# The merge, the output projection and the top-64 of a transformer block: products moved from GpSimd to DVE, last chunks held back, three sorted lists merged

## Chip, cores and metric

The kernel runs on one core of a Trainium2 chip. The metric is the device time of one execution in microseconds (us), the median of several. The engines are named as the profile names them: PE multiplies matrices, DVE (VectorE) and ACT (ScalarE) work on tiles, POOL is GpSimd, SP issues most of the DMAs.

## What is computed

One layer of a diffusion backbone on 512 latent tokens of 1024 channels with 256 context tokens. Two attention branches are projected, gated, added and projected once more; then comes a layer norm, a router, and a mixture of 16 experts in which each expert takes its 64 best tokens.

```python
y = gates[..., :D_MODEL] * (o_mla @ w_o_mla) + gates[..., D_MODEL:] * (o_diff @ w_o_diff)
o_lat = y @ w_out
x = layer_norm(DEEPNORM_ALPHA * x + g1 * o_lat, ln1_g[l], ln1_b[l])
h = x * (1.0 + sc2) + sh2
aff = jax.nn.softmax((h @ w_router + b_router).astype(jnp.float32), axis=-1)
g, idx = lax.top_k(jnp.swapaxes(aff, 1, 2), cap)          # cap = 64 of 512 tokens, 16 experts
hid = silu(xe @ w1) * (xe @ w3);  ye = hid @ w2           # xe = h[idx], then ye * g is added back
x = layer_norm(DEEPNORM_ALPHA * x + g2 * moe, ln2_g[l], ln2_b[l])
```

## The kernel before

All products of the projections are made of three matmuls, since each operand is split into a high part and a rest (`mm3`, lines 80 to 84; `split`, lines 72 to 78: ACT writes the high part, DVE the rest). A scheduler puts the instructions of all engines in order, except PE's in the expert stage, where the order is the program's.

**The merge** (lines 897 to 912) walks over eight groups `j` of 128 channels. PE makes `om`, the MLA branch's projection, by 12 matmuls from `oM` and the split weights `ohi`, `olo`. DVE multiplies it with its gate into `gy` (L907). POOL adds the other branch, which lies gated in `th`, into `ys` (L909). ACT takes the high part `yh` (L910), DVE the rest `yl` (L911).

**The output projection** (lines 1001 to 1035) has two halves `hf` of 512 output channels, and in each four tiles `t` of 128 tokens. A tile is 24 matmuls into `po`: eight chunks `k` of the contraction, three matmuls each; chunk `k` needs `yh` and `yl` of group `k`. The weights come as `outraw`, and are split into `woh` and `wol` (`w_out_split`). In the first half DVE multiplies `po` with the modulation `g1b` into `r` (L1012) and adds the scaled residual into `xn` (L1013). In the second half POOL has multiplied the weights `outraw` with `g1b` before their split (L893), so DVE needs only L1013. `g1b` is spread over the partitions by two matmuls (L118) and two copies on ACT (L119). PE then transposes `xn` (L1016) and makes the router's logits `lgT` and `lg`; these stand in PE's order among the next tile's matmuls. In the second half each tile's chain goes on over DVE, POOL and ACT to its softmax `aff`.

**The top-64** (lines 985 to 1056): a tile's `aff` is transposed by PE to 16 rows, one for each expert (`columns`). `largest` takes eight rounds, each a MAX8 (the eight largest of a row, L989) and a MATCH_REPLACE8 that strikes them out (L991; the profile shows it with a MATCH_VALUE_LOAD ahead). Tiles 0 and 1 together make 256 columns, whose 64 largest are put ahead of the 256 columns of tiles 2 and 3; the second sort runs over these 320. The smallest of the 64 is the threshold; its broadcast `vb` (L1061) and two compares give the slots of the tokens, and the expert stage can begin.

**The expert stage** streams 201 MB of weights `moe_w` through a ring of pages in SBUF (`prefetch`, L941, issued by SP). A page is loaded again when PE has used it up. Some pages of the ring lie in memory that the merge and the projection use before.

Of the kernel before, what the change touches and what calls it, by code (L numbers as in the profile page):

```python
# [29 lines left out]
E_N = 16  # L30
# [8 lines left out]
MOD_AT = ((1, 4), (), (), (0, 1, 3), (0, 1, 3))  # L39
PARTS = (0, 384, 2), (384, 384, 2), (768, 256, 4)  # L40
BN_W = 128
T_SETS = ((0, 1), (2, 3))
D_PARTS, M_PARTS, D_TR, M_TR = 4, 4, 5, 1


# [7 lines left out]
def _layer(tc, A, out, opened):  # L53
# [835 lines left out]
        wraw[hf, kk] = raw  # L889

    def w_out_split(hf, kk):
        if hf:
            G.tensor_tensor(wraw[hf, kk], wraw[hf, kk], g1b[:, None, 512:].to_broadcast([128, 2, 512]), op=OP.mult)  # L893
        split(woh[hf][kk], wol[hf][kk], wraw.pop((hf, kk)))

    for c in range(2, 4):
# [3 lines left out]
    for c in range(4):  # L900
        hl = wos[c]
        for jj in range(2):
            j = 2 * c + jj
            ps = psc.tile([128, 512], F32, name="om", bufs=4)
            wo_mul(ps, hl, jj, oM)
            g = yt.tile([128, 512], F32, name="gy")
            V.scalar_tensor_tensor(g, th[j], 1.0, ps, op0=OP.add, op1=OP.mult)  # L907
            ys = yt.tile([128, 512], F32, name="ys")
            G.tensor_tensor(ys, g, th[KD + j], op=OP.add)  # L909
            S.activation(yh[:, j, :], ys, AF.Copy, scale=0.5)  # L910
            V.scalar_tensor_tensor(yl[:, j, :], ys, 0.5, f(yh[:, j, :]), op0=OP.mult, op1=OP.subtract)  # L911
        w_out_split(0, c)
# [53 lines left out]
    rM, _ = pool("rM", side="right")  # L966
    xn = [rM.tile([128, D], F32, name=f"xn{t}") for t in range(NT)]
    slt = rM.tile([128, NT, E_N], F32, name="slt")
    aff = rM.tile([128, NT, E_N], F32, name="aff")

    g1b = rM.tile([128, D], F32, name="g1b", tag="gb", bufs=1)
    for g in range(2):
        spread(g1b[:, g * 512:(g + 1) * 512], 0, 32 * g, psc.tile([128, 512], F32, name="om", bufs=4))
    mp, close_mp = pool("modp", side="left")
    for t in range(NT):
        dma(xn[t], xr[:, t, :])
# [3 lines left out]
    bst = [mp.tile([128, 2, 6], F32, name=f"bst{t}") for t in range(NT)]  # L980
    wrw = wrp.rearrange("p k e -> p (k e)")
    la0 = [mp.tile([128, E_N], F32, name=f"la{t}") for t in range(NT)]
    top = mp.tile([E_N, CAP], F32, name="top")

    def largest(src, w, dst, last=False):

# [6 lines left out]
    def columns(dst, c0, ts):

        ps = psc.tile([128, 512], F32, name="om", bufs=4)
        for i, t in enumerate(ts):
            T.transpose(ps[:E_N, i * 128:(i + 1) * 128], aff[:, t, :], ident)
            V.tensor_copy(dst[:, c0 + i * 128:c0 + (i + 1) * 128], ps[:E_N, i * 128:(i + 1) * 128])

    cand = [mp.tile([E_N, 128 * len(ts) + (CAP if i else 0)], F32, name=f"cand{i}") for i, ts in enumerate(T_SETS)]  # L1000
    for hf in range(2):
        hs = slice(hf * 512, (hf + 1) * 512)
        for t in range(NT):
            tsl = slice(t * 128, (t + 1) * 128)
            ps = psc.tile([128, 512], F32, name="po", bufs=2)
            for k in range(KD):
                mm3(ps, yh[:, k, tsl], yl[:, k, tsl],
                    woh[hf][k // 2][:, k % 2, :], wol[hf][k // 2][:, k % 2, :], k == 0, k == KD - 1)
            r = ps
            if hf == 0:  # L1010
                r = mp.tile([128, 512], F32, name="r", bufs=2)
                V.tensor_tensor(r, ps, g1b[:, hs], op=OP.mult)  # L1012
# [12 lines left out]
            lgs = mp.tile([128, 128], F32, name="lgs", bufs=1)
            S.activation(lgs, lgT[:, :128], AF.Copy)
# [12 lines left out]
            rsqrt(mv[:, 2:3], mv[:, 1:2], 1.0, 1)  # L1039
            V.scalar_tensor_tensor(la0[t], la0[t], mv[:, 2:3], brt, op0=OP.mult, op1=OP.add)  # L1040
            la = mp.tile([128, E_N], F32, name="la", bufs=2)
            V.scalar_tensor_tensor(la, lg[:, :E_N], mv[:, 2:3], la0[t], op0=OP.mult, op1=OP.add)
            sm_ = mp.tile([128, 4], F32, name="sm_", bufs=2)
            V.tensor_reduce(sm_[:, 0:1], la, axis=AX.X, op=OP.max, negate=True)
            S.activation(la, la, AF.Exp, bias=sm_[:, 0:1], accum_out=sm_[:, 1:2])
            V.reciprocal(sm_[:, 2:3], sm_[:, 1:2])
            V.tensor_scalar(aff[:, t, :], la, sm_[:, 2:3], None, op0=OP.mult)
            V.scalar_tensor_tensor(mv[:, 3:4], mv[:, 0:1], -1.0, mv[:, 2:3], op0=OP.mult, op1=OP.mult)
            G.tensor_scalar(xn[t], xn[t], mv[:, 2:3], mv[:, 3:4], op0=OP.mult, op1=OP.add)
            for i, ts in enumerate(T_SETS):  # L1050
# [6 lines left out]
    vb = psc.tile([128, 512], F32, name="om", bufs=4)  # L1060
# [293 lines left out]
```

## Time and profile before

| | us |
|---|---|
| median of 3 runs (1062.12 to 1064.32) | 1063.86 |
| the profiled execution's own time | 1062.01 |
| its span | 1060.2 |
| PE busy, DVE busy, ACT busy, POOL busy | 981.3, 451.9, 277.9, 201.5 |
| merge begins on PE, projection's last matmul begins, expert stage's first matmul begins | 465.37, 555.45, 572.15 |

Busy times are sums over the whole span; an engine can be busy and still wait at the place that counts. The times of single instructions are counted from the span's start. "[9.37 <-DVE xn L1013]" behind an instruction means that its engine was idle for 9.37 us before it and that the named instruction ended the wait.

### The profile page before, as it was taken

The numbers are of one execution on the slowest core, as the hardware profiler recorded it, in microseconds if no ns is written. First come the engines' busy times: TensorE is split into PE (matmuls) and PEld (weight loads), VectorE is DVE, ScalarE is ACT, GpSimd is POOL, SyncE is SP. The second block draws the span as 40 slices with busy tenths as digits, with TensorE's granted clock in tenths as the row PEclk, the third lists the DMA queues.
The fourth block names the chain that finished last, engine by engine and source line by source line (L and its number), as shares of the span: only waits on it lengthen the run. The fifth ranks groups of instructions, "written<-read, shape, count | busy, mean of one in ns | idle before, by whom it ended". The sixth has DMA issues, their size and how long they took to land.

```text
span 1060.2 us, 13786 instructions
## 1 busy us (share of the span) xinstructions
PE 981.3 (93%) x5267; PEld 617.0 (58%) x5267; DVE 451.9 (43%) x831; ACT 277.9 (26%) x555; POOL 201.5 (19%) x189
## 2 busy tenths in 40 slices
PE   6999998989989999998795999999999999999992
PEld 5888977768778777775563453535353534324331
DVE  2373366652678565547555413131313131111227
ACT  2222424224776555534110011010101001010010
POOL 2340020201667322226111500000000000000004
PEclk9999998999999999999896999999999999999996
DMA  9943346752112000047757979999999999999993
GB/s 296 310 145 117 91 142 238 239 185 61 29 32 65 31 20 2 20 138 273 272 203 306 337 302 409 409 409 409 409 409 409 409 409 409 409 409 408 409 373 119
DMA packets 101210, 266.97 MB, mean 252 GB/s; under 512 B 14021, under 2 KB 37529, under 8 KB 101145
## 3 DMA queue, kind: packets, MB, share of 16 engines
q1 hardware_dynamic: 100248, 264.52, 67.2%
q0 software_dynamic: 320, 1.05, 0.4%
q8 instruction: 41, 0.67, 0.3%
q10 hardware_dynamic: 576, 0.52, 0.1%
q14 instruction: 25, 0.20, 0.1%
HBM read 261.47 MB, written 2.10 MB: 249 GB/s over the span
## 4 chain that ended last, share of the span: by engine, by line
PE 66%; DMA 17%; DVE 8%; POOL 3%; issue 3%; ACT 2%; SPq 0%; POOLq 0%; DVEq 0%; ACTq 0%
PE h L1146 14%; DMA wr<-moe_w 12%; PE y L1162 9%; PE mx L1109 6%; PE acc L84 5%; PE acc L83 5%; PE acc L82 5%; PE sc L653 4%; DMA wa<-w_ada 4%; PE tpb L661 3%; PE av L841 2%; PE mx L1175 2%; PE tp L237 1%; PE av L777 1%; DVE wol L78 1%
## 5 line engine op out<-in xcount | busy, mean ns | idle before, releaser
L1146 PE MATMUL h<-wr,xe 128*64 128x512 f32 x1024 | 233.8, 598 | 8.8 <-DMA wr<-moe_w 7.1
L1146 PEld LDWEIGHTS h<-wr,xe 128*64 128x64 f32 x1024 | 68.2, 137 | 163.1 <-issue 106.5
L1162 PE MATMUL y<-wr,hidT 128*64 128x512 f32 x448 | 97.7, 594 | 0.0
L642 DVE TENSOR_REDUCE nm<-sc 128x1 f32<-128x768 f32 x64 | 61.0, 953 | 36.0 <-PE sc L653 35.5
L1121 POOL TENSOR_TENSOR oh<-oh,aff 128x512 f32<-128x512 f32 x8 | 8.4, 1047 | 353.2 <-PE mx L1109 353.2
L1149 DVE TENSOR_TENSOR hid<-hid,h 128x512 f32<-128x512 f32 x16 | 11.0, 687 | 145.6 <-PE h L1146 145.6
L1162 PEld LDWEIGHTS y<-wr,hidT 128*64 128x64 f32 x448 | 31.5, 137 | 61.8 <-issue 57.9
L643 ACT ACTIVATE P<-sc,nm 128x768 f32<-128x768 f32 x64 | 57.6, 900 | 31.9 <-DVE nm L642 22.9
L1109 PE MATMUL mx<-oh,xn 128*128 128x128 f32 x512 | 61.4, 283 | 1.4 <-DVE oh L1099 1.4
L1109 PEld LDWEIGHTS mx<-oh,xn 128*128 128x128 f32 x512 | 60.3, 199 | 2.5 <-issue 2.1
L75 ACT ACTIVATE whi<-wraw 128x1024 fp32r<-128x1024 f32 (+1 forms) x32 | 33.5, 1047 | 98.3 <-DMA wraw<-w_in 62.9
L78 DVE TENSOR_TENSOR wlo<-wraw,whi 128x1024 fp32r<-128x1024 f32 (+1 forms) x32 | 39.1, 1222 | 45.5 <-PE acc L83 30.0
L75 ACT ACTIVATE ye<-y 128x512 fp32r<-128x512 f32 (+2 forms) x17 | 9.7, 572 | 178.6 <-DVE y L1169 98.7
L82 PE MATMUL acc<-xlh,whi 128*128 128x512 f32 x128 | 50.9, 398 | 2.8 <-ACT whi L75 2.8
L1176 DVE TENSOR_TENSOR acc<-acc,mx 128x512 f32<-128x512 f32 x56 | 34.7, 680 | 41.4 <-PE mx L1175 41.4
L1148 ACT ACTIVATE hid<-h 128x512 f32<-128x512 f32 x16 | 9.6, 597 | 157.5 <-PE h L1146 157.5
L82 PE MATMUL acc<-whi,xlh 128*128 128x512 f32 (+1 forms) x128 | 49.6, 391 | 1.2 <-ACT whi L75 1.2
L83 PE MATMUL acc<-xll,whi 128*128 128x512 f32 x128 | 50.1, 391 | 0.0
L84 PE MATMUL acc<-xlh,wlo 128*128 128x512 f32 x128 | 49.5, 394 | 0.6 <-DVE wlo L78 0.5
L1169 DVE SCALAR_TENSOR_TENSOR y<-y,gate,g2b 128x512 f32<-128x512 f32 x14 | 9.9, 754 | 92.6 <-PE y L1162 92.6
L84 PE MATMUL acc<-whi,xll 128*128 128x512 f32 (+1 forms) x128 | 48.7, 381 | 0.5 <-POOL xll L78 0.5
L83 PE MATMUL acc<-wlo,xlh 128*128 128x512 f32 (+1 forms) x128 | 48.8, 381 | 0.1
(336 smaller groups left out, 1737.1 us busy)
## 6 DMA issues: line engine op xcount, KB each, us to landing
wr<-moe_w SPq DMA_DIRECT2D x372, 512.0 KB, 10.2
wa<-w_ada SPq DMA_DIRECT2D x32, 512.0 KB, 4.5
wraw<-w_in SPq DMA_DIRECT2D x28, 512.0 KB, 4.7
wa<-w_ada SPq DMA_DIRECT2D x8, 1024.0 KB, 9.2
wr<-moe_w SPq DMA_DIRECT2D x16, 384.0 KB, 8.5
outraw<-w_out SPq DMA_DIRECT2D x8, 512.0 KB, 10.2
xq<-x SPq DMA_DIRECT2D x4, 512.0 KB, 7.9
q<-q SPq DMA_DIRECT2D x16, 128.0 KB, 2.3
```

The costliest lines, as they stand in the source:

```text
L75: S.activation(hi, src, AF.Copy)
L78: (eng_lo or V).tensor_tensor(lo, src, f(hi), op=OP.subtract)
L82: T.matmul(ps, lh, rh, start=start, stop=False)
L83: T.matmul(ps, lh, rl, start=False, stop=False)
L84: T.matmul(ps, ll, rh, start=False, stop=stop)
L642: V.tensor_reduce(nm, ps[:, :768], axis=AX.X, op=OP.max, negate=True)
L643: S.activation(p, ps[:, :768], AF.Exp, bias=nm, accum_out=z)
L653: T.matmul(ps[:, a:b], l, r[:, a:b], start=i == 0, stop=i == len(passes) - 1)
L1109: T.matmul(pss[hf][:, kk * 128:(kk + 1) * 128], xn[t][:, k * 128:(k + 1) * 128], o[:, t].rearrange("p e s -> p (e s)"), start=t == 0, stop ...
L1146: T.matmul(ph[i][64 * hf:64 * hf + 64, :], xe[:, k, sl], w[:, hf * 512:(hf + 1) * 512], start=k == 0, stop=k == KD - 1)
L1162: T.matmul(py[hf][r0:r0 + 64, :], hT[:, e % 2, fc % 4, fc // 4, :], w[:, hf * 512:(hf + 1) * 512], start=fc == 0, stop=fc == KD - 1)
L1176: V.tensor_tensor(acc[t][:, hs], acc[t][:, hs], ps, op=OP.add)
```

## The change

POOL's two kinds of products go to DVE: `ys` (L909) becomes a DVE instruction, and the multiplication of the second half's weights by `g1b` (L893) is dropped, while all eight tiles now get the multiplication `r` when DVE takes them out of `po`. For the first two tiles PE multiplies chunks 0 to 6 of both, then spreads `g1b`, and only then does chunk 7 of each; `po` has three PSUM banks now and `om` three instead of four. The top-64 is made of three sorts instead of two: tiles 0 and 1 side by side (64 rows of 128 columns, two blocks of 32 rows, of which 16 are used), then tile 2 together with the 64 survivors of the first sort (192 columns), and tile 3 alone (128 columns). Two sorted lists of 64 are merged by the maximum of one list and the other read backwards: the 64 results are the 64 largest of both, in no order. The threshold is the smallest of the last merge (a TENSOR_REDUCE).

```diff
     def w_out_split(hf, kk):
-        if hf:
-            G.tensor_tensor(wraw[hf, kk], wraw[hf, kk], g1b[:, None, 512:].to_broadcast([128, 2, 512]), op=OP.mult)
         split(woh[hf][kk], wol[hf][kk], wraw.pop((hf, kk)))
...
-            G.tensor_tensor(ys, g, th[KD + j], op=OP.add)
+            V.tensor_tensor(ys, g, th[KD + j], op=OP.add)
...
-    aff = rM.tile([128, NT, E_N], F32, name="aff")
+    affp = rM.tile([128, NT, 32], F32, name="aff")
+    aff = affp[:, :, :E_N]
+    V.memset(affp[:, :, E_N:], 0.0)
...
-    for g in range(2):
-        spread(g1b[:, g * 512:(g + 1) * 512], 0, 32 * g, psc.tile([128, 512], F32, name="om", bufs=4))
...
+        if t == 1:
+            T.transpose(ps[:64, :128], affp[:, 0:2, :].rearrange("p t e -> p (t e)"), ident)
+            V.tensor_copy(cand01, ps[:64, :128])
+            largest(cand01, 128, l01)
+
+            S.activation(cand2[:, :CAP], l01[32:32 + E_N, ::-1], AF.Copy)
+            V.tensor_tensor(cand2[:, :CAP], cand2[:, :CAP], l01[:E_N], op=OP.max)
+            return
+        dst = cand2[:, CAP:] if t == 2 else cand3
+        T.transpose(ps[:E_N, :128], aff[:, t, :], ident)
+        V.tensor_copy(dst, ps[:E_N, :128])
+        if t == 2:
+            largest(cand2, CAP + 128, l2)
+        else:
+            largest(cand3, 128, l3, True)
...
+            if (hf, t) not in pos:
+                pos[hf, t] = psc.tile([128, 512], F32, name="po", bufs=3)
+                if (hf, t) == (0, 0):
+
+                    pos[0, 1] = psc.tile([128, 512], F32, name="po", bufs=3)
+                    for t_ in range(2):
+                        out_mul(pos[0, t_], 0, t_, range(KD - 1))
+                    for g in range(2):
+                        spread(g1b[:, g * 512:(g + 1) * 512], 0, 32 * g, psc.tile([128, 512], F32, name="om", bufs=3))
+                else:
+                    out_mul(pos[hf, t], hf, t, range(KD - 1))
+            ps = pos.pop((hf, t))
+            out_mul(ps, hf, t, range(KD - 1, KD))
+            r = mp.tile([128, 512], F32, name="r", bufs=2)
+            V.tensor_tensor(r, ps, g1b[:, hs], op=OP.mult)
             V.scalar_tensor_tensor(xn[t][:, hs], xn[t][:, hs], ALPHA, r, op0=OP.mult, op1=OP.add)
...
-    for i, ts in enumerate(T_SETS):
-        nxt_ = top if i + 1 == len(T_SETS) else cand[i + 1][:, 0:CAP]
-        largest(cand[i], 128 * len(ts) + (CAP if i else 0), nxt_, i + 1 == len(T_SETS))
+    V.tensor_tensor(l2, l2, l3[:, ::-1], op=OP.max)
+    top = mp.tile([E_N, 1], F32, name="top")
+    V.tensor_reduce(top, l2, axis=AX.X, op=OP.min)
```

The order that the scheduler makes of it moves at three places. First DVE from the end of the merge to the first tile taken out of `po` (numbers behind names tell buffers apart). Before:

```order
L907 SCALAR_TENSOR_TENSOR gy_4480<-th14_708,om_4467 128x512
L911 SCALAR_TENSOR_TENSOR yl_4296<-ys_4463,yh_4295 128x512
L911 SCALAR_TENSOR_TENSOR yl_4296<-ys_4482,yh_4295 128x512
L78 TENSOR_TENSOR wol_4520<-outraw_4517,woh_4519 128x1024
L78 TENSOR_TENSOR wol_4524<-outraw_4521,woh_4523 128x1024
L1012 TENSOR_TENSOR r_4617<-po_4592,g1b_4503 128x512
L78 TENSOR_TENSOR wol_4528<-outraw_4525,woh_4527 128x1024
L1013 SCALAR_TENSOR_TENSOR xn0_4497<-xn0_4497,r_4617 128x512
L78 TENSOR_TENSOR wol_4532<-outraw_4529,woh_4531 128x1024
```

And in the changed kernel:

```order
L904 SCALAR_TENSOR_TENSOR gy_4480<-th14_708,om_4467 128x512
L908 SCALAR_TENSOR_TENSOR yl_4296<-ys_4463,yh_4295 128x512
L906 TENSOR_TENSOR ys_4482<-gy_4480,th15_709 128x512
L908 SCALAR_TENSOR_TENSOR yl_4296<-ys_4482,yh_4295 128x512
L968 MEMSET aff_4502 128x4x16
L77 TENSOR_TENSOR wol_4515<-outraw_4512,woh_4514 128x1024
L77 TENSOR_TENSOR wol_4519<-outraw_4516,woh_4518 128x1024
L77 TENSOR_TENSOR wol_4523<-outraw_4520,woh_4522 128x1024
L77 TENSOR_TENSOR wol_4527<-outraw_4524,woh_4526 128x1024
L1042 TENSOR_TENSOR r_4641<-po_4588,g1b_4504 128x512
L1042 TENSOR_TENSOR r_4667<-po_4589,g1b_4504 128x512
L1043 SCALAR_TENSOR_TENSOR xn0_4497<-xn0_4497,r_4641 128x512
```

All four `wol` of the second half now stand ahead of the first `r`, and no product of POOL stands ahead of any of them. Second, PE around the transposes of the first tile of `xn`. Before they stand inside the second tile, behind 15 of its 24 matmuls:

```order
L82 MATMUL po_4641<-woh_4322,yh_4295 128x512
L83 MATMUL po_4641<-wol_4323,yh_4295 128x512
L84 MATMUL po_4641<-woh_4322,yl_4296 128x512
L1016 MATMUL om_4620<-ident_58,xn0_4497 128x128 x4
L82 MATMUL po_4641<-woh_4322,yh_4295 128x512
```

In the changed kernel they stand in the third tile (`po_4690`), behind 7 of its matmuls, and those of the second tile of `xn` follow at once:

```order
L83 MATMUL po_4589<-woh_4326,yl_4296 128x512
L81 MATMUL po_4690<-woh_4314,yh_4295 128x512
L82 MATMUL po_4690<-wol_4315,yh_4295 128x512
L83 MATMUL po_4690<-woh_4314,yl_4296 128x512
L81 MATMUL po_4690<-woh_4314,yh_4295 128x512
L82 MATMUL po_4690<-wol_4315,yh_4295 128x512
L83 MATMUL po_4690<-woh_4314,yl_4296 128x512
L81 MATMUL po_4690<-woh_4318,yh_4295 128x512
L1046 MATMUL om_4644<-ident_58,xn0_4497 128x128 x4
L1046 MATMUL om_4670<-ident_58,xn1_4498 128x128 x4
```

So PE has 16 matmuls more to do before it needs the first `xn`. Third, DVE at the end of the last tile, where the passes of the sorts stand between the chain's instructions. Before the last sort has DVE for itself:

```order
L1047 TENSOR_SCALAR aff_4502<-la_5034,sm__5036 128x16
L998 COPY cand1_4591<-om_5043 16x128
L989 MAX top_4589<-cand1_4591 16x8
L991 MATCH_REPLACE cand1_4591<-top_4589,cand1_4591 16x320
L989 MAX top_4589<-cand1_4591 16x8
```

In the changed kernel:

```order
L1077 TENSOR_SCALAR aff_4502<-la_5075,sm__5077 128x16
L985 MAX l01_4586<-cand2_4585 16x8
L1012 COPY cand01_4584<-om_5084 16x128
L987 MATCH_REPLACE cand2_4585<-l01_4586,cand2_4585 16x192
L985 MAX l3_4587<-cand01_4584 16x8
L985 MAX l01_4586<-cand2_4585 16x8
L987 MATCH_REPLACE cand01_4584<-l3_4587,cand01_4584 16x128
L987 MATCH_REPLACE cand2_4585<-l01_4586,cand2_4585 16x192
```

The second sort (`cand2`) is still under way when the last list (`cand01`, first 16 rows) arrives: its first five rounds and the sixth MAX stand between the instructions of the last tile's chain, the rest among the passes of the last list.

## Rows read from the trace of the kernel before

**Rows 1.** The chain of work that ended last (start us, us, what), expert stage.
```profile
855.05 4.21 PE h L1146 x19
859.26 10.18 DMA wr<-moe_w
```

**Rows 2.** Busy time by stretch: engines in us, granted clock of PE, DMA share, GB/s.
```profile
477.00:494.00 17.00, 16.77 (x72) 12.44 (x70) 13.79 (x16) 6.96 (x9) 9.17 (x6) 1.00 0.74 282
501.00:510.00 9.00, 1.08 (x5) 1.09 (x6) 8.96 (x7) 2.82 (x3) 6.18 (x2) 0.57 1.02 407
614.00:620.00 6.00, 6.00 (x57) 6.00 (x55) 1.52 (x5) 0.70 (x2) 0.11 (x1) 1.00 0.76 302
620.00:626.00 6.00, 6.00 (x27) 2.04 (x27) 1.21 (x4) 1.79 (x3) 0.94 (x1) 1.00 0.30 98
626.00:632.00 6.00, 6.00 (x32) 2.01 (x30) 0.00 (x0) 0.00 (x0) 0.00 (x0) 1.00 0.99 343
900.00:1033.00 133.00, 125.46 (x586) 46.55 (x582) 29.56 (x63) 11.68 (x23) 1.47 (x2) 1.00 1.03 402
```

**Rows 3.** Waits of PE, 463 to 640: us in total, times, longest.
```profile
PE om L1016 <- DVE xn L1013: 10.2, 2, 9.4
PE om L1061 <- DVE top L989: 8.5, 1, 8.5
...
PE po L84 <- DVE yl L911: 0.4, 1, 0.4
PE po L82 <- ACT yh L910: 0.2, 1, 0.2
```

**Rows 4.** Timeline of PE (start us, us), end of the merge and projection.
```profile
487.96 1.13 PE L118 MATMUL om<-rm,one 1*128 1x512 f32 x4
...
499.16 0.39 PE L84 MATMUL po<-woh,yl 128*128 128x512 f32 x1
508.92 1.11 PE L1016 MATMUL om<-ident,xn 128*128 128x128 f32 x4 [9.37 <-DVE xn L1013]
...
520.30 0.39 PE L83 MATMUL po<-wol,yh 128*128 128x512 f32 x1
520.52 0.39 PE L84 MATMUL po<-woh,yl 128*128 128x512 f32 x1
```

**Rows 5.** Groups by line, 463 to 580: xcount, busy us, mean ns, idle before.
```profile
L78 DVE TENSOR_TENSOR wol<-outraw,woh 128x1024 fp32r<-128x1024 f32 x8 | 16.4, 2067 | 3.9 <-ACT woh L75 3.9
...
L893 POOL TENSOR_TENSOR outraw<-outraw,g1b 128x1024 f32<-128x1024 f32 x4 | 11.3, 2856 | 1.7 <-ACT g1b L119 1.7
...
L989 DVE MAX8 top<-cand 16x8 f32<-16x320 f32 x8 | 3.9, 482 | 0.3
...
L989 DVE MAX8 cand<-cand 16x8 f32<-16x256 f32 x8 | 3.3, 413 | 0.1
...
L78 DVE TENSOR_TENSOR olo<-oraw,ohi 128x1024 fp32r<-128x1024 f32 x2 | 2.4, 1218 | 0.0
```

**Rows 6.** Timeline of DVE (start us, us), projection to the end of the sorts.
```profile
499.40 5.57 DVE L78 TENSOR_TENSOR wol<-outraw,woh 128x1024 fp32r<-128x1024 f32 x2 [3.85 <-ACT woh L75]
504.90 0.68 DVE L1012 TENSOR_TENSOR r<-po,g1b 128x512 f32<-128x512 f32 x1
...
514.04 0.69 DVE L1012 TENSOR_TENSOR r<-po,g1b 128x512 f32<-128x512 f32 x1 [0.62 <-PE po L84]
514.76 0.69 DVE L1013 SCALAR_TENSOR_TENSOR xn<-xn,r 128x512 f32<-128x512 f32 x1
...
520.95 0.69 DVE L1012 TENSOR_TENSOR r<-po,g1b 128x512 f32<-128x512 f32 x1 [2.44 <-PE po L84]
...
555.88 0.69 DVE L1013 SCALAR_TENSOR_TENSOR xn<-xn,po 128x512 f32<-128x512 f32 x1
...
561.41 0.48 DVE L989 MAX8 top<-cand 16x8 f32<-16x320 f32 x1
...
569.06 0.48 DVE L989 MAX8 top<-cand 16x8 f32<-16x320 f32 x1
```

More of the change, by code (lines that the diff above doesn't have):

```diff
@@ L41 @@
 BN_W = 128
-T_SETS = ((0, 1), (2, 3))
 D_PARTS, M_PARTS, D_TR, M_TR = 4, 4, 5, 1
@@ L903, in _layer @@
             j = 2 * c + jj
-            ps = psc.tile([128, 512], F32, name="om", bufs=4)
+            ps = psc.tile([128, 512], F32, name="om", bufs=3)
             wo_mul(ps, hl, jj, oM)
@@ L982, in _layer @@
     la0 = [mp.tile([128, E_N], F32, name=f"la{t}") for t in range(NT)]
-    top = mp.tile([E_N, CAP], F32, name="top")
     def largest(src, w, dst, last=False):
@@ L991, in largest, with columns, out_mul @@
                 V.match_replace(out=src[:, :w], in_to_replace=m8, in_values=src[:, :w], imm_value=-1.0)
[L993 to L1000, printed above, removed]
+    cand01 = mp.tile([64, 128], F32, name="cand01")
+    cand2 = mp.tile([E_N, CAP + 128], F32, name="cand2")
+    cand3 = cand01[:E_N]
+    l01 = mp.tile([64, CAP], F32, name="l01")
+    l2 = l01[:E_N]
+    l3 = mp.tile([E_N, CAP], F32, name="l3")
+    def columns(t):
+        if t == 0:
+            return
+        ps = psc.tile([128, 512], F32, name="om", bufs=3)
+        if t == 1:
[4 more added lines that the diff above has]
+            V.tensor_tensor(cand2[:, :CAP], cand2[:, :CAP], l01[:E_N], op=OP.max)
+            return
+        dst = cand2[:, CAP:] if t == 2 else cand3
[5 more added lines that the diff above has]
+            largest(cand3, 128, l3, True)
+    def out_mul(ps, hf, t, ks):
+        tsl = slice(t * 128, (t + 1) * 128)
+        for k in ks:
+            mm3(ps, yh[:, k, tsl], yl[:, k, tsl],
+                woh[hf][k // 2][:, k % 2, :], wol[hf][k // 2][:, k % 2, :], k == 0, k == KD - 1)
+    pos = {}
     for hf in range(2):
@@ L1003, in _layer @@
         for t in range(NT):
[L1004 to L1012, printed above, removed]
+            if (hf, t) not in pos:
[12 more added lines that the diff above has]
+            V.tensor_tensor(r, ps, g1b[:, hs], op=OP.mult)
             V.scalar_tensor_tensor(xn[t][:, hs], xn[t][:, hs], ALPHA, r, op0=OP.mult, op1=OP.add)
-            ps = psc.tile([128, 512], F32, name="om", bufs=4)
+            ps = psc.tile([128, 512], F32, name="om", bufs=3)
             for k in range(4):
@@ L1049, in _layer @@
             G.tensor_scalar(xn[t], xn[t], mv[:, 2:3], mv[:, 3:4], op0=OP.mult, op1=OP.add)
-            for i, ts in enumerate(T_SETS):
-                if ts[-1] == t:
-                    columns(cand[i], CAP if i else 0, ts)
-    for i, ts in enumerate(T_SETS):
-        nxt_ = top if i + 1 == len(T_SETS) else cand[i + 1][:, 0:CAP]
-        largest(cand[i], 128 * len(ts) + (CAP if i else 0), nxt_, i + 1 == len(T_SETS))
-    vb = psc.tile([128, 512], F32, name="om", bufs=4)
-    T.transpose(vb[:, :E_N], top[:, CAP - 1:CAP].to_broadcast([E_N, 128]), ident[:E_N, :E_N])
+            columns(t)
+    V.tensor_tensor(l2, l2, l3[:, ::-1], op=OP.max)
+    top = mp.tile([E_N, 1], F32, name="top")
+    V.tensor_reduce(top, l2, axis=AX.X, op=OP.min)
+    vb = psc.tile([128, 512], F32, name="om", bufs=3)
+    T.transpose(vb[:, :E_N], top.to_broadcast([E_N, 128]), ident[:E_N, :E_N])
     mk = mp.tile([128, NT, 2, E_N], BF16, name="mk")
@@ L1064, in _layer @@
         V.tensor_tensor(mk[:, :, i, :], aff, vb[:, None, :E_N].to_broadcast([128, NT, E_N]), op=op)
-    ps = psc.tile([128, 512], F32, name="om", bufs=4)
+    ps = psc.tile([128, 512], F32, name="om", bufs=3)
     pc = ps[:, :2 * NT * E_N].rearrange("p (t i e) -> p t i e", i=2, e=E_N)
```

## The prediction

> **What bounds the kernel now.** I read the chain of waits first. From 859 us on it goes over the loads of the expert weights [rows 1]: PE has caught up with the stream, and the kernel ends when the last page has landed and been used. The stream itself is read from the busy times by stretch: from 626 us to its end at 1033 us it is never idle, at a share of 0.99 and more and some 400 GB/s [rows 2]. Just ahead of that it has gaps: in 614 to 626 us its share is 0.76 and 0.30, so 1.4 + 4.2 = 5.6 us are idle, while PE is fully busy. There SP holds the next load until PE has used up a page. So the end hangs on the stream, the stream's last stop hangs on PE in the first expert pairs, and PE gets there by the path of this change: merge, projection, top-64. What this path gains, the releases of pages gain, and so the end, as long as the stream is not late already.
>
> Then the waits of PE on that path [rows 3]. Two are long: 9.4 us before the transposes of the first `xn`, and 8.5 us before the threshold's broadcast. The first is a wait behind others: PE has done 15 matmuls of the second tile at 499.5 us and then stands until 508.92 [rows 4], because the first `xn` on DVE stands behind `r`, and `r` behind two `wol` that take 5.57 us after a wait of 3.85 [rows 6] for ACT's `woh`, which in turn waits for POOL's products `outraw`. These take 2.86 us each, four in a row, and cannot begin before `g1b` is there; beside them a `wol` takes 2.07 us in the mean, where the same split `olo` takes 1.22 without POOL [rows 5].
>
> **The path's terms**, against the profiled execution's own 1062.0 us.
>
> *The wait of 9.4 us goes.* In the merge PE is not held up: 8 x 12 matmuls at 0.23 us (the spacing in [rows 4]) are 22.4 us from 465.4, so `om` ends at 488. Then come 42 matmuls (chunks 0 to 6 of two tiles, 9.8 us), the spread (1.1 us [rows 4], as before, only later) and 6 matmuls: the second tile is done near 500.4, and the 7 matmuls ahead of the first transposes last until 502.0. DVE needs, after its last `yl`, four `wol` of 1.22 us. I put the last `yl` at 493: `gy`, `ys`, ACT's `yh` and `yl` of the last group follow `om` by some 0.7 us each, and DVE has about 2 us of other splits still in hand. ACT's four `woh` run just ahead of the `wol`, so DVE is free at 498.5, and waits for PE. Then `r` and `xn` of tile 0 take 0.7 us each with the second `r` between them: 500.0 + 2.1 = 502.1, against PE's 502.0. Kept wait 0 to 1 us, I take 0.1. The cover is 1.5 us of DVE's idle time; what it costs if that is gone is rival A.
>
> *The slow clock behind it goes: -1.7.* In 501 to 510 us the granted clock is 0.57 [rows 2], which is 1.2 GHz for most of it, after PE had stood idle. From 508.92 to the next `r` at 514.04 are 9 matmuls and one tile's transposes and logits. At full clock a tile of 24 matmuls with them takes 520.95 - 514.04 = 6.91 [rows 6], so this piece would take 6.91 - 15 x 0.23 = 3.46 instead of 5.12.
>
> *The small waits go: -0.6.* PE waits 0.4 us for `yl` and 0.2 for `yh` [rows 3] at the last chunks of the first tile; now chunk 7 comes 11 us after `om`'s end.
>
> *Nothing for tiles 2 to 7.* DVE gets four more `r` (0.69 us each) in the second half, in tiles that take PE 6.9 us, and PE reaches a tile's transposes 7 matmuls into the next tile, 1.6 us after the tile's end; `r` and `xn` take 0.72 + 0.69 [rows 6]. That fits by 0.2 us; a pass of the sort between them eats it, at one tile.
>
> *The last tile: +0.7 and +1.0.* Behind the last matmul no cover is left. `r` ahead of `xn` costs its 0.72. The chain to the list's copy takes 561.41 - 555.88 = 5.5 us before. Now five rounds of the second sort stand in it. The bounds are 0 (they fill DVE's waits for PE, ACT and POOL) and their whole time. A round of 320 columns takes (569.06 - 561.41) / 7 = 1.09 us [rows 6]; MAX8 falls from 482 to 413 ns for 64 columns less [rows 5] and the strike-out alike, so a round of 192 is about 0.82 and one of 128 about 0.69, and five are 4.1 us at most. The chain's own waits are longer than that in sum, but a pass of 0.3 us begun just before a value arrives delays it. I take 1.0, nearer to 0.
>
> *The last sort: -0.5.* Before 8.1 us (561.41 to 569.54). Now 7 x 0.69 + 0.3 = 5.1, the leftover two and a half rounds of the second list 2.1, and the merge with the minimum 0.4: 7.6.
>
> The page "VectorE: DVE Perf Modes" of the Trainium skill (section on the TRN2 errata) says that a DVE instruction pays a fixed time whatever its length, and advises long ones. The rows have it: 482 against 413 ns leaves about 0.2 us when the columns are taken to nothing. If a short pass were no cheaper than one of 256 columns (0.96 a round by the same slope), the last term would be +1.8 instead of -0.5.
>
> Three sorts have 24 MAX8 where two had 16. The first, 8 x 0.69 = 5.5 us, runs between the chains of the seventh tile while PE multiplies on, 6.9 us to a tile, and costs nothing but the few tenths above; without that cover it would cost its 5.5.
>
> Sum: -9.4 + 0.1 - 1.7 - 0.6 + 0.7 + 1.0 - 0.5 = -10.4. The profiled execution would take 1051.6 us. The median shown is 1.9 above it, and the three runs spread over 2.2; I forecast **1052.5 us**, between 1051.6 and 1053.5. What a measurement of this kernel can tell from no change is about 0.2%, 2.1 us.
>
> **Rivals.**
>
> *A. DVE becomes the merge's bound (13 in 100).* In 477 to 494 us DVE is busy for 13.79 of 17 us [rows 2] and gets eight `ys` more. The Trainium skill ("Perfetto Trace Analysis", Optimizing Scalar/DVE Operations) says that work may be moved off a saturated DVE; this change moves it on. The rows have DVE at 0.81, near to that but not there. If DVE waits out each round trip to ACT (0.7 us, eight times), its 24 passes of 0.69, ten splits of 1.22 and these waits are 34.4 us from 468.5: `r` would begin at 503, `xn` come at 505, and PE wait 3 us and lose the clock for some 1.7: 1057. Against it: DVE's order has another group's pass to do during most of these trips, and POOL no longer stretches the splits.
>
> *B. The stream does not move in full (6 in 100).* If the earlier loads kept their times, only the 5.6 us of idle time before 626 us could be taken out: 1052.5 + 4.8 = 1057.3; if those gaps stayed too, 1062. Against it: the loads in them wait for PE, which is earlier.
>
> *C. The tail eats more (6 in 100).* All five rounds delay the last chain (+3.1) and short passes cost as long ones (+2.3): 1058.
>
> *D. Slower (3 in 100).* In the second half each `xn` comes late, PE stops in every tile, and the clock stays at 1.2 GHz, as it did after the stop at 499.5. With matmuls twice as long a tile would take 24 x 0.46 + 2 = 13 us, 6.1 more; two tiles eat the gain, six give 1052.5 + 37 = 1089. It decides by whether PE's wait in a tile grows from tenths to microseconds. Against it: from 510 us on PE runs without a stop with the same chain, less one pass.
>
> **Numbers.** The forecast has 72 in 100. A, B and C all end near 1057 and still faster; D and a stream that does not move at all (2 of B's 6) are not. The range has to hold the kept wait (0 to 1), the last tile's passes (0 to 4.1), the last sort (-0.5 to +1.8), the runs' spread of 2.2 and most of rival A: 1049.5 to 1057.5. Faster by more than 0.2% 0.95, within 0.2% 0.02, slower 0.03.
>
> **What would show it.** In the changed profile PE's wait for `xn` (9.4) is below 1 us and the clock near 500 us full; `wol` of the second half takes 1.2 us; `om` ends at 488 as before, the last projection matmul begins near 544 instead of 555.5, the broadcast near 559 instead of 569.6; the stream's last gap ends near 616 instead of 626, and the stream ends 10 us earlier. The forecast is wrong if PE still waits for more than 2 us before 510, if the broadcast follows the last matmul by more than 16 us (14.1 before), or if the stream's end moves by less than the broadcast.

## The result, and the profile after

The changed kernel takes **1049.65 us** (median of 4 runs, 1047.56 to 1050.75), the kernel before 1063.09 beside it (4 runs): a ratio of 0.9871, 95% interval 0.9851 to 0.989. By the ratio that is 13.7 us less. The forecast was 1052.5, between 1051.6 and 1053.5, in a range of 1049.5 to 1057.5. The gain came out some 2 to 3 us larger than forecast: the time lies below the narrower bounds and just inside the range. The two profiled executions (spans 1060.2 and 1045.8 us) differ by 14.4 us. Cut at the same places, in us, with a second profiled execution of the changed kernel (span 1046.4, from the experiments):

| stretch | before | forecast | after | after, 2nd |
|---|---|---|---|---|
| start to the merge's first matmul | 465.37 | 465.37 | 463.92 | 463.54 |
| to the projection's last matmul | 90.08 | 78.5 | 77.80 | 77.83 |
| to the copy of the last list | 5.65 | 7.35 | 7.73 | 7.39 |
| to the broadcast of the threshold | 8.50 | 8.0 | 6.89 | 6.90 |
| to the expert stage's first matmul | 2.55 | 2.55 | 2.58 | 2.59 |
| to its first product `h` | 6.87 | 6.87 | 5.76 | 6.67 |
| to the end | 481.18 | 481.18 | 481.12 | 481.48 |

The last row says that the whole gain of the path reaches the end. The waits of PE from 463 to 640 us, changed kernel (us in total, times, longest), beside [rows 3]:

```profile
PE om L1089 <- DVE top L1083: 6.9, 1, 6.9
PE om L1011 <- DVE aff L1077: 2.2, 1, 2.2
PE om L1046 <- DVE xn L1043: 1.6, 1, 1.6
```

The wait of 9.4 us before the first `xn` is gone, and so are those for `yl` and `yh`. What is left of the waits for `xn` (L1046) is the last tile's. The timeline of PE, changed kernel (start us, us):

```profile
463.92 0.50 PE L81 MATMUL om<-oM,ohi 128*128 128x512 f32 x1
...
486.42 0.39 PE L81 MATMUL po<-woh,yh 128*128 128x512 f32 x1
...
500.21 1.24 PE L1046 MATMUL om<-ident,xn 128*128 128x128 f32 x8
...
541.72 0.40 PE L83 MATMUL po<-woh,yl 128*128 128x512 f32 x1
543.75 0.66 PE L1046 MATMUL om<-ident,xn 128*128 128x128 f32 x4 [1.63 <-DVE xn L1043]
...
549.03 0.38 PE L1011 MATMUL om<-ident,aff 128*16 128x128 f32 x1 [2.21 <-DVE aff L1077]
556.34 0.28 PE L1089 MATMUL om<-ident,top 16*128 16x16 f32 x1 [6.93 <-DVE top L1083]
...
558.92 5.18 PE L1137 MATMUL mx<-oh,xn 128*128 128x128 f32 x32 [1.19 <-DVE oh L1127]
564.68 5.80 PE L1174 MATMUL h<-wr,xe 128*64 128x512 f32 x26 [0.57 <-DVE xe L1142]
```

PE stands nowhere between 463.92 and 541.72, the first transposes included. Behind the projection's last matmul its longest waits until the broadcast are those for `xn`, for `aff` and for the threshold `top`. The first 32 matmuls of the expert stage, `mx`, in the kernel before, from the stretch that the forecast left alone:

```profile
572.15 6.29 PE L1109 MATMUL mx<-oh,xn 128*128 128x128 f32 x32 [1.19 <-DVE oh L1099]
```

The same 32 matmuls took 6.29 us before and 5.18 after. DVE of the changed kernel, from the last `yl` to the threshold, beside [rows 6]:

```profile
490.73 0.69 DVE L908 SCALAR_TENSOR_TENSOR yl<-ys,yh 128x512 fp32r<-128x512 f32 x1 [0.70 <-ACT yh L907]
...
491.68 4.63 DVE L77 TENSOR_TENSOR wol<-outraw,woh 128x1024 fp32r<-128x1024 f32 x4 [0.19 <-ACT woh L74]
498.20 1.31 DVE L1042 TENSOR_TENSOR r<-po,g1b 128x512 f32<-128x512 f32 x2 [1.88 <-PE po L83]
...
549.45 0.28 DVE L1012 COPY cand<-om 16x128 f32<-16x128 f32 x1 [0.23 <-PE om L1011]
549.65 0.07 DVE L987 MATCH_VALUE_LOAD cand<-l,cand 16x8 f32 x1
549.72 0.33 DVE L987 MATCH_REPLACE8 cand<-l,cand 16x192 f32<-16x192 f32 x1
549.99 0.53 DVE L985 MAX8 l<-cand 16x8 f32<-16x128 f32 x2
...
552.07 0.27 DVE L985 MAX8 l<-cand 16x8 f32<-16x128 f32 x1
...
556.08 0.21 DVE L1083 TENSOR_REDUCE top<-l 16x1 f32<-16x64 f32 x1
```

Four `wol` now take 4.63 us together, where two took 5.57 [rows 6], and DVE has 1.88 us to spare before `r`. From 549.65 to 552.07 the rest of the second list's sort and two rounds of the last list alternate. Groups by line, 463 to 580 us, changed kernel (xcount, busy us, mean ns), beside [rows 5]:

```profile
L77 DVE TENSOR_TENSOR wol<-outraw,woh 128x1024 fp32r<-128x1024 f32 x8 | 9.4, 1219 | 0.2 <-ACT woh L74 0.2
L985 DVE MAX8 l<-cand 16x8 f32<-16x192 f32 x8 | 2.7, 338 | 0.0
L985 DVE MAX8 l<-cand 16x8 f32<-16x128 f32 x8 | 2.2, 278 | 0.2
```

The `wol` are back at the time of an undisturbed split, and MAX8 falls with the columns. Busy time by stretch, changed kernel (PE, PEld, DVE, ACT, POOL, PE's granted clock, DMA share, GB/s), beside [rows 2]:

```profile
477.00:494.00 17.00, 17.00 (x76) 13.80 (x75) 15.31 (x22) 10.49 (x13) 0.00 (x0) 1.00 0.75 270
501.00:510.00 9.00, 9.00 (x60) 6.45 (x62) 3.33 (x7) 2.17 (x5) 0.00 (x0) 1.00 1.03 410
557.00:561.00 4.00, 2.74 (x18) 2.61 (x19) 1.29 (x5) 0.00 (x0) 0.00 (x0) 0.50 1.03 410
561.00:565.00 4.00, 3.42 (x26) 3.11 (x27) 0.78 (x3) 1.28 (x1) 0.00 (x0) 0.90 0.70 279
...
602.00:606.00 4.00, 4.00 (x37) 3.83 (x36) 1.79 (x6) 0.06 (x1) 0.45 (x1) 1.00 0.51 205
606.00:610.00 4.00, 4.00 (x16) 1.32 (x18) 0.87 (x3) 1.73 (x3) 0.59 (x1) 1.00 0.10 15
610.00:614.00 4.00, 4.00 (x21) 1.29 (x18) 0.00 (x0) 0.00 (x0) 0.00 (x0) 1.00 0.92 320
```

The stream's last gap lies in 602 to 610 us, where before it lay in 614 to 626 [rows 2]: it moved with PE.

### The profile page after: what moved, and what is told of

Its sections match the earlier page's. It is cut to its first block, busy times and chain, and to the rows that moved or that the text cites. A ratio compares the mean times of both kernels' runs of the same rounds, so it can differ in the third digit from the quotient of the medians.

```text
span 1045.8 us, 13799 instructions
## 1 busy us (share of the span) xinstructions
PE 977.7 (93%) x5266; PEld 614.1 (59%) x5266; DVE 451.9 (43%) x870; ACT 278.2 (27%) x556; POOL 176.1 (17%) x177
## 3 DMA queue, kind: packets, MB, share of 16 engines
q0 software_dynamic: 320, 1.05, 0.4%
## 4 chain that ended last, share of the span: by engine, by line
PE 72%; DMA 16%; DVE 7%; ACT 2%; issue 2%; POOL 2%; SPq 0%; DVEq 0%; ACTq 0%; POOLq 0%
PE h L1174 16%; DMA wr<-moe_w 10%; PE y L1190 9%; PE mx L1137 6%; PE acc L83 5%; PE acc L82 5%; PE acc L81 5%; PE sc L652 4%; PE tpb L660 3%; DMA wa<-w_ada 3%; PE av L840 3%; PE mx L1203 2%; DMA wraw<-w_in 2%; PE tp L236 2%; PE po L83 1%
## 5 line engine op out<-in xcount | busy, mean ns | idle before, releaser
L74 ACT ACTIVATE whi<-wraw 128x1024 fp32r<-128x1024 f32 (+1 forms) x32 | 33.5, 1046 | 99.4 <-DMA wraw<-w_in 75.4
```

What stands on the lines that cost most here:

```text
L74: S.activation(hi, src, AF.Copy)
```

## The experiments

Times vary by 2 us and more from run to run, so each part is read from its stretch: *A* from the merge's first matmul to the projection's last (before 90.08, after 77.80 and 77.83 us), *B* from there to the broadcast (14.15; 14.62 and 14.29), *C* from the expert stage's first matmul to the first `h` (6.87; 5.76 and 6.67). Ratios are to the kernel before, with their 95% intervals.

### products_alone: the kernel before, with only the products moved

```diff
-        if hf:
-            G.tensor_tensor(wraw[hf, kk], wraw[hf, kk], g1b[:, None, 512:].to_broadcast([128, 2, 512]), op=OP.mult)
...
-            G.tensor_tensor(ys, g, th[KD + j], op=OP.add)
+            V.tensor_tensor(ys, g, th[KD + j], op=OP.add)
...
-            r = ps
-            if hf == 0:
-                r = mp.tile([128, 512], F32, name="r", bufs=2)
-                V.tensor_tensor(r, ps, g1b[:, hs], op=OP.mult)
+            r = mp.tile([128, 512], F32, name="r", bufs=2)
+            V.tensor_tensor(r, ps, g1b[:, hs], op=OP.mult)
```

> The kernel before with only the products moved: ys on DVE, no weights times g1b on POOL, r for all eight tiles; spread, tile order and both sorts as before. Theory (the products are the cause of the 9.4 us wait): the wait before the first xn shrinks to about 1 us, because three wol instead of four slow ones stand ahead of that xn; no slow clock near 500 us; from the last projection matmul to the broadcast 14.15 + 0.85 = 15.0 us, since r stands in the last tile's chain; the time is 1 to 2 us above the changed kernel, some 1051. Rival (holding back the last chunks is the cause): the wait stays at 4 us or more, the clock falls behind it, and the time is 1055 to 1058.

Measured: 1051.1 us, ratio 0.9901 (0.9876 to 0.9926); A 77.68, B 15.83. PE's timeline has no stop before the first `xn`, and its longest wait for `xn` is the last tile's:

```profile
499.33 0.66 PE L1012 MATMUL om<-ident,xn 128*128 128x128 f32 x4
...
546.32 0.66 PE L1012 MATMUL om<-ident,xn 128*128 128x128 f32 x4 [2.03 <-DVE xn L1009]
```

The products alone take away the whole of the long wait; the 1 us that I expected to be left is not there. B is 0.8 longer than expected, because passes of the 256-column sort stand in the last tile's chain: a MAX8 of 0.41 us ahead of `r`, a strike-out of 0.40 us with its load between `r` and `xn`.

### not_held: the changed kernel without the last chunks held back

```diff
+    for g in range(2):
+        spread(g1b[:, g * 512:(g + 1) * 512], 0, 32 * g, psc.tile([128, 512], F32, name="om", bufs=3))
...
-            if (hf, t) not in pos:
...
-            out_mul(ps, hf, t, range(KD - 1, KD))
+            ps = psc.tile([128, 512], F32, name="po", bufs=3)
+            out_mul(ps, hf, t, range(KD))
```

> The changed kernel without the last chunks held back: g1b is spread ahead of the projection, and the tiles of the first half are multiplied one after the other. Theory (with the products on DVE nothing is late any more, so holding back buys nothing): from the merge's first matmul to the last projection matmul 77.8 us, within 0.4 of the changed kernel; time within 1 us. Rival (it covers DVE's splits): PE waits 1 us or more for the first xn or for yl, 79 us or more.

Measured: 1048.38 us, ratio 0.9853 (0.9835 to 0.9872); A 78.02, B 14.61. Multiplying the last chunks behind is worth 0.2 us of A here, and nothing of the time. The rival falls.

### ys_on_pool and weights_on_pool: one product back on POOL

```diff
-            V.tensor_tensor(ys, g, th[KD + j], op=OP.add)
+            G.tensor_tensor(ys, g, th[KD + j], op=OP.add)
```

> The changed kernel with ys back on POOL. Theory (ys is no part of the gain): the last yl is 2 to 3 us later than in the changed kernel, four wol of 1.2 us follow, and PE waits 0.5 to 1.5 us for the first xn with the clock at its upper level; within 1.5 us of the changed kernel. Rival (ys on POOL stretches DVE's passes and is half of the gain): a wait of 3 us or more before the first xn, time 5 us above the changed kernel.

Measured: 1052.45 us, ratio 0.991 (0.9889 to 0.9932); A 80.31, B 15.05. A grew by 2.5 us, more than expected and at another place: PE stops not at the first `xn` but at the seventh chunk of the first tile (waits of PE):

```profile
PE po L81 <- ACT yh L907: 1.5, 1, 1.5
...
PE po L83 <- DVE yl L908: 0.4, 1, 0.4
```

From 488.71 us, the start of the matmul ahead of these two waits, to 492.06, that of the one behind them, are four steps: they take 3.35 us where four at 0.23 take 0.9, and these 2.4 us are nearly all of the 2.5. So the theory that `ys` is no part of the gain falls, and so does the rival's half of it.

```diff
+        if hf:
+            G.tensor_tensor(wraw[hf, kk], wraw[hf, kk], g1b[:, None, 512:].to_broadcast([128, 2, 512]), op=OP.mult)
...
-            r = mp.tile([128, 512], F32, name="r", bufs=2)
-            V.tensor_tensor(r, ps, g1b[:, hs], op=OP.mult)
+            r = ps
+            if hf == 0:
+                r = mp.tile([128, 512], F32, name="r", bufs=2)
+                V.tensor_tensor(r, ps, g1b[:, hs], op=OP.mult)
```

> The changed kernel, but POOL multiplies the second half's weights by g1b again, and r is made for the first half alone. Theory (the four products on POOL, which cannot begin before g1b, are the cause of the old wait, since wol and with them xn stand behind them on DVE): the first xn is on time, but a wol that waits for POOL stands ahead of the second xn; PE waits 2 to 4 us there, and the last tile is 0.85 us shorter without r; 1 to 4 us above the changed kernel. Rival (the last chunks held back are enough, since the second half's weights are due only at 525 us): no wait above 1 us, and the time is 1 us below the changed kernel's.

Measured: 1054.34 us, ratio 0.9929 (0.9906 to 0.9951); A 83.75, B 13.31. The timeline of POOL has the four products in one row:

```profile
498.26 11.27 POOL L892 TENSOR_TENSOR outraw<-outraw,g1b 128x1024 f32<-128x1024 f32 x4 [40.27 <-DMA xn<-x]
```

That of DVE shows what runs beside them:

```profile
499.29 1.92 DVE L1047 SCALAR_TENSOR_TENSOR xn<-xn,r 128x512 f32<-128x512 f32 x1
501.78 2.74 DVE L77 TENSOR_TENSOR wol<-outraw,woh 128x1024 fp32r<-128x1024 f32 x1 [0.57 <-ACT woh L74]
```

That of ACT shows `woh` waiting for POOL and `hT` behind it:

```profile
500.69 1.06 ACT L74 ACTIVATE woh<-outraw 128x1024 fp32r<-128x1024 f32 x1 [2.51 <-POOL outraw L892]
503.47 1.06 ACT L74 ACTIVATE woh<-outraw 128x1024 fp32r<-128x1024 f32 x1 [1.72 <-POOL outraw L892]
504.43 0.58 ACT L1052 ACTIVATE hT<-om 128x512 f32<-128x512 f32 x1
```

And that of PE two of the waits that follow, for `xn` and for `hT`:

```profile
501.26 0.66 PE L1050 MATMUL om<-ident,xn 128*128 128x128 f32 x4 [1.03 <-DVE xn L1047]
505.06 0.53 PE L1057 MATMUL lgT<-hT,wrg 128*32 128x128 f32 x8 [2.22 <-ACT hT L1052]
```

As expected the four products do the harm even with the chunks held back and the first `xn` on time, though by 6 us of A and not by 2 to 4, and in a way that I had not listed: ACT's `woh` waits for POOL, and `hT` stands behind it. A third wait for `xn`, of 0.80 us, comes at 515 us, and from 505 to 509 us the granted clock is 0.57. Beside POOL's product an `xn` of 0.69 us takes 1.92. The rows say how: this `xn` ends at 501.21 and the `wol` at 504.52, 0.52 and 1.05 us after the start of the `woh` that POOL's product released (500.69 and 503.47). The next `xn` and `wol` end 0.52 and 1.05 us after theirs as well. So these passes look held until POOL's product has ended, and not slowed in proportion; no run tests this by itself. B is 1.0 to 1.3 us shorter without the last tile's `r`, about the 0.85 expected.

With the chunks held back, taking `ys` back costs 2.5 us of A and taking the weights back 6.0, together 8.5 of the 12.3 us. How the rest divides between the two, and what holding the chunks back is worth while POOL still makes the products, no run shows.

### sorts_alone, two_sorts and one_after_another: the top-64

`sorts_alone` is the kernel before with the change's `columns` and merges; `two_sorts` is the changed kernel with the same piece taken back:

```diff
-    for i, ts in enumerate(T_SETS):
-        nxt_ = top if i + 1 == len(T_SETS) else cand[i + 1][:, 0:CAP]
-        largest(cand[i], 128 * len(ts) + (CAP if i else 0), nxt_, i + 1 == len(T_SETS))
+    V.tensor_tensor(l2, l2, l3[:, ::-1], op=OP.max)
+    top = mp.tile([E_N, 1], F32, name="top")
+    V.tensor_reduce(top, l2, axis=AX.X, op=OP.min)
```

> The kernel before with only the three sorts in place of two. Theory (passes of two lists that do not depend on each other overlap on DVE, so the last sort is 1.6 us shorter, not 0.5, while the rounds of the second list cost the last tile's chain 1.2): from the last projection matmul's start to the broadcast 14.15 - 0.4 = 13.75 us, of it 6.9 from the last copy of a list to the broadcast; the wait of 9.4 us stays; time 1062.5 to 1063. Rival (the terms as predicted, +1.0 and -0.5): 14.65 us, 7.9 from the copy to the broadcast. Rival (a short pass costs as much as a long one): over 10 us from the copy to the broadcast, time 1065.

Measured: 1061.71 us, ratio 0.9994 (0.9972 to 1.0015); B 13.30, of it 6.54 from the last copy to the broadcast. The forecast's terms (14.65) fall, and so does a short pass that costs as much as a long one.

> The changed kernel with the two sorts of before (256 columns, then 320). Theory: the first xn has no wait, as in the changed kernel; from the last copy of a list to the broadcast 8.5 us instead of 6.9, the last tile's chain 0.4 to 1.2 us shorter than in the changed kernel; from the last projection matmul's start to the broadcast 15.0 instead of 14.6; the time within 1 us of the changed kernel's. Rival (the sorts bring the surplus over the forecast): 2 us or more above the changed kernel.

Measured: 1051.09 us, ratio 0.9892 (0.9868 to 0.9917); A 77.60, B 15.47, of it 8.50 from the copy. The sorts are worth 0.9 to 1.2 us of B in either kernel; the time does not tell this from nothing. Nor does it decide against the rival: beside `changed_again` the median is 2.8 us higher, by the ratios 1.4 us, and the intervals overlap. The test of why the last sort is so short is one line:

```diff
-    cand3 = cand01[:E_N]
+    cand3 = cand2[:, :128]
```

> The changed kernel with the last list in the second list's memory, so that its copy and its eight rounds begin only when the second sort is over. Theory (where the rounds of two lists alternate, a pass does not wait for the end of the one before it, and that is the 1.1 us by which the last sort was shorter than forecast): from the last transposition of aff to the broadcast 8.2 to 8.6 us instead of 7.3; the time 1 us above the changed kernel. Rival (the rounds are shorter whatever stands beside them): 7.3 to 7.6 us.

Measured: 1050.28 us, ratio 0.9895 (0.987 to 0.992); from the last transposition of `aff` to the broadcast 8.38 us. The wait of PE for the threshold, which was 6.9 us:

```profile
PE om L1089 <- DVE top L1083: 8.0, 1, 8.0
```

And the timeline of DVE, the copy of the last list, its first round and the threshold:

```profile
554.73 0.28 DVE L1012 COPY cand<-om 16x128 f32<-16x128 f32 x1
555.05 0.28 DVE L985 MAX8 l<-cand 16x8 f32<-16x128 f32 x1
555.36 0.08 DVE L987 MATCH_VALUE_LOAD cand<-l,cand 16x8 f32 x1
555.44 0.26 DVE L987 MATCH_REPLACE8 cand<-l,cand 16x128 f32<-16x128 f32 x1
555.74 0.28 DVE L985 MAX8 l<-cand 16x8 f32<-16x128 f32 x1
...
560.46 0.21 DVE L1083 TENSOR_REDUCE top<-l 16x1 f32<-16x64 f32 x1
```

Behind one another a round is 0.69 us, as forecast; the load begins 0.03 us after the end of the MAX8, and the next MAX8 0.04 us after the end of the strike-out. Alternating, two MAX8 together were 0.53 us, and the passes in 549.65 to 552.07 took 2.42 us: two rounds at 0.69 and two and a half at 0.82 would be 3.4. That difference of 1.0 is, within 0.1, what this kernel loses (8.38 against 7.31 and 7.32 us in the two executions of the changed kernel).

### changed_again: the changed kernel once more

> The changed kernel once more, beside the others. Theory (of the 14.4 us between the two profiled executions, 1.45 lie ahead of the merge and 1.1 in the clock behind the threshold's wait, and both vary from one execution to the next): the merge begins between 463.5 and 466.5 us, the median of the runs is 1048.5 to 1050.5, and the first 32 matmuls of the expert stage with the wait behind them take 5.2 to 6.9 us. Rival (the earlier start of the merge belongs to the change): the merge begins at 463.9 again, within 0.3.

Measured: 1048.3 us (ratio 0.9879, 0.9854 to 0.9904), merge from 463.54, C 6.67. By itself the merge's start speaks for the rival; but over all the profiled executions it lies between 462.19 (`not_held`) and 468.17 us (`kept_busy_shorter`), programs with the same work ahead of it. So a shift of 1.45 between two executions can't be laid to the change. C varies as expected; the median lies just below the 1048.5 to 1050.5 expected.

### kept_busy, kept_busy_shorter: PE's clock behind the last waits

```diff
+    def turn(a, n):
+        for _ in range(n):
+            T.matmul(wm[0][:, :128], a, a, start=True, stop=True)
...
+                turn(r[:, :128], 6)
...
+    turn(xn[3][:, 128:256], 36)
     V.tensor_tensor(l2, l2, l3[:, ::-1], op=OP.max)
```

> The changed kernel with 58 matmuls of 128x128 on PE whose result nobody reads, put into its waits of the last tile and of the threshold (6 ahead of the last xn transposes, 4 and 12 behind them, 36 ahead of the broadcast). Theory (behind these waits the clock is at 1.2 GHz until about 2 us after the expert stage's first matmul, and this is lost time): the granted clock stays at 1.00 in 545 to 560 us, the first 32 matmuls of the expert stage with the wait behind them take 4.2 us instead of 5.8 to 6.9, from the last projection matmul to the broadcast 14.0 instead of 14.3 to 14.6, and the time is 2 to 3 us below the changed kernel's. Rival (the added matmuls stand in PE's order and hold up what comes behind them): from the last projection matmul to the broadcast 15.5 us or more, no gain.

Measured: 1049.17 us, ratio 0.9876 (0.9851 to 0.9902); C 4.39, B 16.17. The rival came: the 36 matmuls took 8.20 us and made the broadcast late, and no gain shows in the time. Of the theory the clock held, and the stretch C with it.

> As kept_busy, with fewer added matmuls (3, 3, 8 and 28), since 36 ran 1.3 us past the threshold. Theory (what was gained on the clock was given back as waiting for the added matmuls): from the last projection matmul to the expert stage's first product h 21.0 to 21.6 us, against 23.0 and 23.6 in the two executions of the changed kernel and 22.9 in kept_busy; 1.5 to 2.5 us below the changed kernel's time. Rival (the added work brings nothing at the end, since the stream of weights sets it): 21.0 to 21.6 us as well, but the stretch from h to the end longer than its 481.1 to 481.5 us by the same amount.

Measured: 1047.23 us, ratio 0.9848 (0.9826 to 0.987); B 14.26, C 4.38, from the projection's last matmul to `h` 20.95, and from `h` to the end 480.86, not longer than in the changed kernel, so the rival falls. Busy time by stretch, through the threshold's wait:

```profile
553.00:557.00 4.00, 4.00 (x36) 3.98 (x37) 3.83 (x21) 0.00 (x0) 0.00 (x0) 1.00 1.02 416
557.00:561.00 4.00, 2.87 (x26) 2.58 (x26) 3.23 (x16) 0.00 (x0) 0.00 (x0) 1.00 1.03 409
```

PE's timeline behind it:

```profile
562.56 3.81 PE L1152 MATMUL mx<-oh,xn 128*128 128x128 f32 x32 [1.20 <-DVE oh L1142]
566.94 3.65 PE L1189 MATMUL h<-wr,xe 128*64 128x512 f32 x15 [0.58 <-DVE xe L1157]
```

The 32 `mx` take 3.81 us at 2.4 GHz; so 1.4 us of the changed kernel's 5.18 and 2.5 of the 6.29 before was the lower clock. In the kernel before the granted clock is 0.50 from 560 to 577 us, but for the first tenths.

### weights_on_dve, and with PE kept busy

```diff
+        if hf:
+            V.tensor_tensor(wraw[hf, kk], wraw[hf, kk], g1b[:, None, 512:].to_broadcast([128, 2, 512]), op=OP.mult)
...
+            r = ps
+            if hf == 0:
...
-                w_out_split(1, t)
+                if t == 1:
+                    spread(g1b[:, 512:], 0, 32, psc.tile([128, 512], F32, name="om", bufs=3))
+                for c in {1: (0, 1), 2: (2,), 3: (3,)}.get(t, ()):
+                    w_out_split(1, c)
```

> The changed kernel with the second half's weights multiplied by g1b again, but on DVE, behind the first two tiles' xn (the second half of g1b is spread there); r for the first half alone. Theory (the four r of the second half cost only the last tile's 0.85 us, and DVE has room for four passes of 1.2 us in the first half): from the merge's first matmul to the last projection matmul 77.8 us, from there to the broadcast 13.3 to 13.8 instead of 14.3 to 14.6; about 0.8 us below the changed kernel. Rival (the passes stand ahead of an r or xn): PE waits for xn in the first half, 79 us or more, no gain.

Measured: 1047.73 us, ratio 0.9858 (0.9837 to 0.988); A 78.55, B 13.62. B fell as expected, but one product stands between an `r` and its `xn`, PE waits 1.0 us there, and A gives the gain back. Neither side is fully right.

> weights_on_dve with the matmuls of kept_busy_shorter (0, 3, 8 and 26). Theory (both gains add): from the last projection matmul to the first h 20.0 to 20.8 us, 2.5 to 3.5 us below the changed kernel's time, 1046 or less. Rival (the smaller part of the added matmuls lets the clock fall): 21.5 us or more.

Measured: 1047.79 us, ratio 0.9854 (0.9837 to 0.987); A 78.54, B 13.30, from the last matmul to `h` 19.99. From the merge's first matmul to the end it takes 579.42 us, against 581.88 and 582.86 in the two executions of the changed kernel. The stretches add as expected; the time, expected at 1046 or less, did not. Both of these versions with PE kept busy are faster than the kernel before; that they beat the changed kernel shows in the stretches, while the intervals of the times overlap.

## Where the prediction held, and which steps failed

The mechanism held: the wait of 9.4 us goes, and the path's gain reaches the end. What failed is the size of three terms, all too small: *the last sort* (-0.5 forecast, -1.6 measured), *the small waits* (-0.6 forecast, about -1.2 measured), and the clock behind the wait for the threshold, which the sum put at nothing (1.1 and 0.2 us came back in the two executions).

*The wait of 9.4 us goes*: right, with the first `xn` on time. The last `yl` ended at 491.4 us and the four `wol` at 496.3, each 1.2 us, so the cover was 1.9 us and not 1.5. The runs add which part does it: the products. The chunks held back, on which the forecast's later arrival of PE at the transposes rested, are not needed. The forecast's 2.07 us for a `wol` beside POOL was misread: it is the mean of all eight, and the two that it names take 5.57 us, 2.8 each [rows 6].

*The slow clock behind it* and *nothing for tiles 2 to 7*: right. From 501 to 510 us the clock is 1.00.

*The small waits, -0.6*: **this term was mis-sized**. The forecast took the idle times 0.2 and 0.4 us, which count from the modelled end of a matmul (0.39 us), while the next one starts after 0.23. In the kernel before:

```profile
493.02 0.39 PE L84 MATMUL po<-woh,yl 128*128 128x512 f32 x1
493.64 0.50 PE L82 MATMUL po<-woh,yh 128*128 128x512 f32 x1 [0.23 <-ACT yh L910]
...
494.76 0.50 PE L84 MATMUL po<-woh,yl 128*128 128x512 f32 x1 [0.40 <-DVE yl L911]
495.10 0.40 PE L82 MATMUL po<-woh,yh 128*128 128x512 f32 x1
```

From 493.02 to 495.10 are four steps, which at 0.23 us take 0.9 and here take 2.1: the two waits cost 1.2 us. The first three terms made -11.6, and A fell by 12.3; 0.6 of the difference of 0.7 is this. The step gave the wrong cause too: the waits are gone without the held chunk (`not_held`), and come back when `ys` is POOL's.

*The last tile, +0.7 and +1.0*: right. It measured +2.1 and +1.7 in the two executions. In `sorts_alone` and `weights_on_pool`, which have the passes in the chain and no `r` in it, it is +1.1. The reason given was wrong: the chain's own waits are not longer than the five rounds' 4.1 us, since the ten passes from `xn` to the list's copy take 3.0 of the 5.5 us in the kernel before.

*The last sort, -0.5*: **this term was mis-sized**; it is -1.6. The rounds were priced rightly (0.69 us), but I added the second list's leftover rounds to those of the last list, as if every pass waited for the one before. They alternate, and 1.0 of the 1.1 us vanishes by it; `one_after_another` has it back. The price that followed from a fixed time per pass (+1.8) is out: MAX8 has 278 ns at 128 columns and 338 at 192. The fixed time of which the Trainium skill speaks ("VectorE: DVE Perf Modes", TRN2 errata) is there in these rows: 60 ns for 64 columns leave 158 ns when the columns are taken to nothing (the forecast's two figures leave 0.14 us, and not its 0.2).

**A term was missing**: I followed the clock behind the wait that goes, not behind the one that stays. In the expert stage's first 32 matmuls it gave 1.1 us back in the profiled execution and 0.2 in the second; it depends on when the clock comes up again, and the runs with PE kept busy show that up to 2.5 us lie there. With 1.1 here, 1.1 from the sort, 0.7 in A and 1.45 ahead of the merge, less 0.4 in the last tile, the profiled execution's 4.0 us below the forecast are accounted for; only the sort and A came again in full.

*Rivals.* A: DVE is busy for 15.31 of 17 us in 477 to 494, more than before, and yet PE never waits there. What the Trainium skill says of a saturated DVE ("Perfetto Trace Analysis", Optimizing Scalar/DVE Operations), that work may be moved off it, did not bind at 0.90. B: from the first `h` to the end all fourteen profiled executions take 480.8 to 481.9 us, with `h` between 563 and 579; the stream moves in full. C and D did not come: the broadcast follows the last matmul after 14.6 us, and no tile's `xn` is late but the last.

## What to carry to other kernels

Look at what stands ahead of the first due instruction in each engine's order: moving eight and four products from a less busy to a busier engine gained 12 us, since the products had held up ACT, and DVE behind it. Price a short wait from start to start of the instructions around it, and not by its idle time alone. Where short passes of two independent lists can alternate on DVE, count them by the time of the pair and not by the sum of two chains. Price the clock behind the waits that stay as well as behind those that go.

## What the runs showed of the hardware

- Beside a POOL product of two tensors, which takes 2.8 us, DVE passes stretch: `xn` from 0.69 to 1.92 us, `wol` from 1.22 to 2.74. They end 0.52 (`xn`) and 1.05 us (`wol`) after the start of the ACT pass that waited for that product, twice each in `weights_on_pool`, as if held until POOL was done. `r`, read from `po`, keeps its 0.68 us at 504.90 in the kernel before [rows 6], beside the same products.
- PE came out of the threshold's wait at 1.2 GHz. It was at 2.4 GHz again some 2.9 us after the expert stage's first matmul in the profiled execution, 4.8 in the second, and 5.2 in the kernel before. 42 added matmuls of 128x128, each two records of 0.12 us, kept it at 2.4 GHz throughout.
- Short DVE passes of two independent lists, alternating, took 2.42 us for four and a half rounds that come to 3.4 us one behind another.
